# Tying ScalarE's order at the start and in the second output phase of a two-layer decoder step

## The chip, the core and the metric

The kernel runs on one core of one Trainium2 chip. The metric is the device time of one execution in microseconds (us), the median of several runs. Besides it there is one profiled execution, from which every duration and wait below is read; it has a time of its own.

The core has five engines with instruction queues of their own: TensorE (PE in the profile; its weight loads are PEld) multiplies matrices, VectorE (DVE), ScalarE (ACT) and GpSimd (POOL) work on elements, and SyncE (SP) issues transfers. ACT issues transfers too. Each engine works through its queue in order and waits on semaphores for the others.

## The reference

Two layers act on 1024 prompt tokens and 8 sample tokens, 1032 columns in all, with a model width of 1024. Cut to what matters here:

```
for i in range(2):                       # layer 0: HGRN2 recurrence, layer 1: gMLP
    hn = rmsnorm(h, norm_mix[i])
    y  = mixer_i(hn)                     # in-projection, mixer, gate, out-projection
    h  = h + y
    gate = sigmoid(rmsnorm(h, norm_ple[i]) @ w_ple_gate[i])
    h  = h + gate * (p[i] @ w_ple_proj[i])
out = rmsnorm(h, norm_final)
rmsnorm(x, g) = x * rsqrt(mean(x * x) + EPS) * g
```

The first rmsnorm squares x itself. The product p[i] @ w_ple_proj[i] needs only inputs, so it can run at any time.

## The kernel before, in words

**Numbers.** All is float32, and every product is made of three matmuls (`mm3`, L201 to L203): each operand is split into a high part (a cast on ACT, L196 for activations and L142 for weights) and a low part (a subtraction on DVE or POOL, L197 and L143).

**Tiling.** The columns are three chunks c = 0, 1, 2 of 384, 384 and 264. A projection of one output block for one chunk (`proj`) is 24 matmuls into one PSUM bank; a group of the p-projection (`pple`) is 6. `proj`, `pple` and the output phase share three banks with the tag "mm". A group of `pple` is copied out by ACT (L301) to a buffer `pple_t`, and a transfer that ACT itself issues (L302) stores it in DRAM (`ppd`). So the fourth group after a copy that is late waits for it.

**What sets the order.** PE's order is the program's order: the scheduler is told to leave PE alone. Small side jobs (the sum matmul `pss` of a norm, its broadcast `pbc`, the transposes `pt_g`) are generators in a clock called `Ticks`: a yield of n means that the next step stands n ticks later, and a tick falls at half of a projection, at its end, or behind `pple` groups. SQD, SDEL and NDEL are such delays. On ACT, DVE, POOL and SP a scheduler chooses the order from its estimates of time, and the order is then fixed.

**Start (0 to 50 us).** p and x are loaded; 12 `pple` groups run; meanwhile `first_norm` (L382 on) squares each chunk of x in four pieces on ACT (L386, POOL adds them for chunks 1 and 2, L387 and L389), `pss` adds over partitions, `pbc` spreads the scale, and DVE writes x times scale (`tmp`, L270), ACT casts it (`bh<-tmp`) and DVE or POOL subtract (`bl`). Then come the projections f (`fk`) and q (`qq`) of the first head, chunk by chunk.

**Layer 0 (to 880), p-projection and gate (to 1058), then the middle (1058 to 1121).** In the middle 12 `pple` groups of layer 1 run under the last gate work, `norm_rows` (NDEL[1]) makes the chunks' norms, `vgroup` applies gelu (L945) to six value projections and puts their transposes (`vstore`, L954) two ticks later, and `mix` combines rows of h on DVE and POOL (L905 to L908) whose casts are `xmh<-h`.

**Units (1121 to 1643), then the second output phase, "ob" (1643 to 1780).** Gated products are stored in `ozd` (L1155), loaded back and split for the output projection `ps_o`. `out_phase` runs the last 12 `pple` groups as filling while its operands come: `load_zt` loads two blocks at a time into three buffers `zstg` and splits each at once (`load_split`, L306). Before that, the last unit loads blocks singly into the tiles `u` (`fetch`) and casts them to `xmh` and `bh`; the fetches (1,4) and (1,8) stand there last, eight single blocks.

The prediction's steps are in `first_norm`, `pple`, `load_zt`, `out_phase` and `vgroup`.

Of the kernel before, what the change touches and what calls it, by code (L numbers as in the profile page):

```python
# [7 lines left out]
F32 = mybir.dt.float32  # L8
# [8 lines left out]
P = 128  # L17
# [12 lines left out]
PRI = 400  # L30
NWARM = 12
FDEL = ((2, 2), (2, 4), (1, 3))
SQD = (0, 5, 9)
OD = (4, 4)
SDEL = ((6, 3), (6, 2), (6, 2))
NDEL = (((1, 3), (1, 4), (2, 3)), ((2, 4), (2, 6), (2, 6)))
OFF = (0, 384, 768)
W = (384, 384, 264)
NT = (3, 3, 2)
# [37 lines left out]
def trunk_kernel(ctx, tc, xT, st, pT, nrm, wina, lbl, gna, wouta, winb, lng, lnb, lngr, lnbr,  # L77
# [7 lines left out]
    def pool(stack, name, bufs=1, **kw):  # L85
        return stack.enter_context(tc.tile_pool(name=name, bufs=bufs, reuse_waits="tile", **kw))
# [105 lines left out]
        return loaded[n]  # L192


    def split(hi, lo, src, eng=V):
        A.copy(hi, src)  # L196
        eng.tensor_tensor(lo, src, hi.bitcast(F32), ALU.subtract)  # L197

    def mm3(ps, wh, wl, xh, xl, first, last, more=False):
# [81 lines left out]
        return ps  # L281


    def load_p(ap, l, c, ph, pl):
        stg = ap.tile([P, 2, 384], F32, name="pstg", bufs=2)
        nc.sync.dma_start(stg[:, :, :W[c]], pT[l][:, :, OFF[c]:OFF[c] + W[c]])
        ph[c] = ap.tile([P, 2, W[c]], F32R, name=f"ph{c}")
        pl[c] = ap.tile([P, 2, W[c]], F32R, name=f"pl{c}")
        split(ph[c], pl[c], stg[:, :, :W[c]], V)

    def pple(l, tp, ph, pl, half, stg):

        wh, wl = take("p", l, half)
        for c in CH:
            for mm in range(4):
                ps = pp.tile([P, 512], F32, name="ps_pple", tag="mm", bufs=3)
                for k in range(2):
# [3 lines left out]
                A.copy(t[:, :W[c]], ps[:, :W[c]])  # L301
# [18 lines left out]
    def run(gen):  # L320
        for _ in gen:
            pass
# [43 lines left out]

    load(0)
    ph, pl = [None] * 3, [None] * 3
    load_p(sp, 0, 0, ph, pl)
    load_p(sp, 0, 1, ph, pl)  # L370
    load_x(0)
    nc.sync.dma_start(ones, cst[1])
    nc.sync.dma_start(ident, cst[0])
    nc.sync.dma_start(g32, nrm)
    load_p(sp, 0, 2, ph, pl)
    load_x(1)
    load(1)
    load_x(2)
# [1 line left out]
    fill = pple(0, sp, ph, pl, 0, ("pple_t", 4))  # L380

    def first_norm(c):  # L382
        yield SQD[c]
        sq = sp.tile([P, KT, 384], F32, name="sq0", bufs=2)[:, :, :W[c]]
        for j in range(0, KT, 2):
            A.activation(sq[:, j:j + 2, :], xs[c][:, j:j + 2, :], AF.Square)  # L386
            (V if c == 0 else G).tensor_tensor(sq[:, j, :], sq[:, j, :], sq[:, j + 1, :], ALU.add)  # L387
            if j:
                (V if c == 0 else G).tensor_tensor(sq[:, 0, :], sq[:, 0, :], sq[:, j, :], ALU.add)  # L389
        yield from norm_proc(sp, sq[:, 0, :], lambda j: xs[c][:, j, :], 0, hh[c], hl[c], c, SDEL[c])  # L390

# [382 lines left out]
    def out_phase(key, zt, ssq, first, done, pre, parts, late, fill=None):  # L774

        with ExitStack() as s:
            zp = pool(s, "oz")

            def load_h(m):
                if m < KT:  # L780
                    src = xT[:, m] if first else hd[m]
                    for c in CH:
                        nc.sync.dma_start(hr[c][m], src[:, OFF[c]:OFF[c] + W[c]])

            st = stage2(pool(s, "zstg"), 3)
            for c, k0, nk in parts:
                zt[c, k0] = (zp.tile([P, nk, W[c]], F32R, name=f"zh{c}_{k0}"),
                             zp.tile([P, nk, W[c]], F32R, name=f"zl{c}_{k0}"), nk)
            todo = load_zt(zt, late, st)
            if fill is not None:  # L790
                for i, _ in enumerate(fill):
                    if i % 2:
                        tk.tick()
                        next(todo, None)
                run(load_zt(zt, [(2, 0)], st))
            run(todo)
            for m in range(4):
                load_h(m)

            def bank():  # L800
                return pp.tile([P, 512], F32, name="ps_o", tag="mm", bufs=3)

            def half(ps, wt, c, hf):
                for _ in out_half(ps, wt, zt, c, hf):
                    tk.tick()

            def add(m, c, ps):
                V.tensor_tensor(hr[c][m], hr[c][m], ps[:, :W[c]], ALU.add)  # L808
                accum_sq(sp, ssq[c], hr[c][m], m == 0, m == KT - 1, W[c])
                if m == KT - 1:  # L810
                    done(c)


            wt = pre["w"] if pre else take(key, 0, 0)
            for c in CH:
                if c not in pre:
                    pre[c] = bank()
                    half(pre[c], wt, c, 0)
            wt = take(key, 1, 0)
            pre1 = [pp.tile([P, 384], F32, name="ps_o1", tag=t, bufs=1) for t in ("pA", "po", "pt")]  # L820
            for c in CH:
                half(pre1[c], wt, c, 0)
            for m, pm in ((0, pre), (1, pre1)):
                wt = take(key, m, 1)
                for c in CH:
                    half(pm[c], wt, c, 1)
                    add(m, c, pm[c])
            for m in range(2, KT):
                wts = [take(key, m, hf) for hf in range(2)]
                load_h(m + 2)  # L830
                for c in CH:
                    ps = bank()
                    for hf in range(2):
                        half(ps, wts[hf], c, hf)
                    add(m, c, ps)
# [103 lines left out]
    def wide():  # L939
        return wb.tile([P, 384], F32, name="u", bufs=6)  # L940

    def vgroup(m, c, src):
        w = W[c]
        gv = wide()
        A.activation(gv[:, :w], src, AF.Gelu_apprx_tanh)  # L945
# [219 lines left out]
    for g in range(8):  # L1165
        us = {}
        unit(take("B", 2 * g), gated(us))
        vn = wb2.tile([P, 8, DV], F32, name="vn", bufs=1)
        nc.sync.dma_start(vn, vraw[g])
        for n in range(8):  # L1170
            V.tensor_scalar(vn[:, n, :], vn[:, n, :], mv[:, n, 0:1], ln["rstd"][:, n:n + 1], ALU.subtract, ALU.mult)
        gb = wb2.tile([P, 2, DV], F32, name="gb", bufs=1)
        nc.sync.dma_start(gb[:, 0, :], lngr[g].partition_broadcast(P))
        nc.sync.dma_start(gb[:, 1, :], lnbr[g].partition_broadcast(P))
        cv = wb2.tile([P, DV], F32, name="cv", bufs=1)
        G.tensor_tensor(cv, vn[:, 7, :], gb[:, 0, :], ALU.mult)
        G.tensor_tensor(cv, cv, gb[:, 1, :], ALU.add)
        nc.sync.dma_start(cv_p[:, g * DV:(g + 1) * DV], cv)
        if g < 7:
            spatial(g, vn, us, take("B", 2 * MI + 2 * g))  # L1180
        else:

            zt = {(0, 0): (hh[0], hl[0], 8), (1, 0): (*xm[1], 4), (1, 4): (*xm[0], 4), (1, 8): (*xm[2], 4),
                  (0, 8): (hh[1], hl[1], 8), (2, 0): (hh[2], hl[2], 8)}
            ph, pl = p_in_act(1, None, False)

            def fetch(c, k0):
                return lambda: run(load_zt(zt, [(c, k0)], lambda w: wide()[:, :w].rearrange("p (k t) -> p k t", k=1), 1))

            spatial(g, vn, us, take("B", 2 * MI + 2 * g),  # L1190
                    (lambda: p_in_act(1, lambda w: ws[0].tile([P, 512], F32, name="ssum", bufs=2)[:, :w]), None, fetch(1, 0), fetch(0, 0), fetch(1, 4),
                     fetch(1, 8)))
# [111 lines left out]
```

## Time and profile before

| | us |
|---|---|
| median of three runs | 1976.65 |
| runs | 1976.61, 1976.65, 1980.89 |
| the profiled execution, its own time | 1973.68 |
| its span (first to last instruction) | 1971.9 |
| TensorE busy | 1893.8 (96%) |
| VectorE, ScalarE, GpSimd busy | 1182.6, 782.9, 456.8 |

The span leaves out 1.78 us of the profiled execution's time (1973.68 - 1971.9). In the profile's rows `L301` is line 301 of the kernel before; "A <- B" means that A's engine sat idle until B released it; a shape as 128x384 is partitions by elements. PEclk is the clock that was granted to TensorE, 1.00 being full speed.

### The profile page before, as it was taken

The page shows a single profiled execution, that of the slowest core. Times are in us where ns is not written, and L with a number is a line of the kernel's source. Part 1 is how long each engine was busy: PE and PEld are TensorE (multiplying, and loading weights), DVE is VectorE, ACT ScalarE, POOL GpSimd, SP SyncE. Part 2 cuts the span into 40 slices and gives each one's busy share as a digit, 9 for nine tenths or more (in the row PEclk, how much of TensorE's full clock was granted, in tenths as well). Part 3 has the DMA queues.
Part 4 walks back from the last instruction along what each step waited for, and adds up shares of the span by engine and source line. Part 5 has one row for each costly group of instructions (what it writes and reads, how often), then busy time and mean ns, then how long its engine had stood idle before and what let it go on. Part 6 is the DMA issues. An engine that isn't in the chain of part 4 may idle for free.

```text
span 1971.9 us, 33475 instructions
## 1 busy us (share of the span) xinstructions
PE 1893.8 (96%) x13160; PEld 1852.3 (94%) x13160; DVE 1182.6 (60%) x2610; ACT 782.9 (40%) x1610; POOL 456.8 (23%) x467
## 2 busy tenths in 40 slices
PE   7999999999999998999998899999999996999997
PEld 6999999999999998999998899999999996999997
DVE  5967676776767676311645755587777675311554
ACT  6452535444453536311434544433443344211341
POOL 5110000001000100011323622354444440011221
PEclk8999999999999999999999899999999998999998
DMA  6232322222131326511243333332233238411123
GB/s 207 84 105 71 101 91 79 76 89 97 57 108 59 106 93 217 185 44 44 98 157 111 108 98 92 102 98 95 97 99 105 95 113 262 138 49 44 65 87 107
DMA packets 124076, 203.73 MB, mean 103 GB/s; under 512 B 11600, under 2 KB 96784, under 8 KB 122896
## 3 DMA queue, kind: packets, MB, share of 16 engines
q1 hardware_dynamic: 115280, 191.04, 29.9%
q10 hardware_dynamic: 8640, 10.57, 1.5%
q8 instruction: 103, 1.69, 0.4%
q14 instruction: 53, 0.43, 0.1%
HBM read 148.75 MB, written 52.82 MB: 102 GB/s over the span
## 4 chain that ended last, share of the span: by engine, by line
PE 45%; DVE 7%; DMA 4%; issue 2%; POOL 2%; ACT 2%; SPq 0%; DVEq 0%; POOLq 0%; ACTq 0%
PE ps_proj L202 7%; PE ps_proj L201 7%; PE ps_proj L203 7%; PE ps_o L201 6%; PE ps_o L202 6%; PE ps_o L203 6%; PE ps_d L201 1%; PE ps_d L203 1%; PE ps_d L202 1%; DMA zstg<-ozd 1%; DVE wlo L143 1%; DMA vn<-vraw 1%; DVE bl L197 1%; PE psp L1139 1%; DMA ppd<-pple_t 1%
## 5 line engine op out<-in xcount | busy, mean ns | idle before, releaser
L201 PE MATMUL ps_proj<-bh,whi 128*128 128x384 f32 (+1 forms) x2136 | 689.2, 323 | 8.1 <-ACT pple_t L301 6.7
L202 PE MATMUL ps_proj<-bl,whi 128*128 128x384 f32 (+1 forms) x2136 | 673.3, 315 | 3.8 <-DVE bl L197 2.5
L203 PE MATMUL ps_proj<-bh,wlo 128*128 128x384 f32 (+1 forms) x2136 | 672.9, 315 | 3.1 <-DVE wlo L143 3.1
L201 PEld LDWEIGHTS ps_proj<-bh,whi 128*128 128x128 f32 x2136 | 404.3, 189 | 12.2 <-ACT pple_t L301 6.9
L202 PEld LDWEIGHTS ps_proj<-bl,whi 128*128 128x128 f32 x2136 | 404.8, 190 | 6.6 <-DVE bl L197 3.4
L203 PEld LDWEIGHTS ps_proj<-bh,wlo 128*128 128x128 f32 x2136 | 403.6, 189 | 3.7 <-DVE wlo L143 3.7
L143 DVE TENSOR_TENSOR wlo<-wstg,whi 128x1024 fp32r<-128x1024 f32 x148 | 190.7, 1289 | 152.1 <-ACT whi L142 148.8
L142 ACT CAST whi<-wstg 128x1024 fp32r<-128x1024 f32 x148 | 155.3, 1050 | 130.0 <-PE ps_proj L202 72.3
L234 POOL TENSOR_TENSOR ssq<-ssq,tmp 128x384 f32<-128x384 f32 (+1 forms) x72 | 76.3, 1059 | 419.9 <-ACT tmp L233 372.2
L808 DVE TENSOR_TENSOR h<-h,ps_o 128x384 f32<-128x384 f32 (+1 forms) x48 | 24.5, 511 | 192.9 <-PE ps_o L203 192.9
L142 ACT CAST shi<-ssum 128x512 fp32r<-128x512 f32 x92 | 56.5, 621 | 176.9 <-POOL ssum L172 102.7
L201 PE MATMUL ps_o<-bh,whi 128*128 128x384 f32 (+1 forms) x384 | 123.2, 321 | 2.1 <-ACT pple_t L301 1.6
L202 PE MATMUL ps_o<-bl,whi 128*128 128x384 f32 (+1 forms) x384 | 122.6, 319 | 0.6 <-DVE bl L197 0.6
L233 ACT ACTIVATE tmp<-h 128x384 f32<-128x384 f32 (+1 forms) x72 | 35.3, 490 | 219.5 <-DVE h L808 168.9
L203 PE MATMUL ps_o<-bh,wlo 128*128 128x384 f32 (+1 forms) x384 | 122.4, 319 | 0.0
L143 DVE TENSOR_TENSOR slo<-ssum,shi 128x512 fp32r<-128x512 f32 x92 | 76.7, 833 | 42.9 <-ACT shi L142 42.9
L201 PE MATMUL ps_o<-zh,whi 128*128 128x384 f32 (+1 forms) x288 | 90.0, 313 | 0.0
L202 PE MATMUL ps_o<-zl,whi 128*128 128x384 f32 (+1 forms) x288 | 89.7, 312 | 0.0
L203 PE MATMUL ps_o<-zh,wlo 128*128 128x384 f32 (+1 forms) x288 | 89.7, 311 | 0.0
L589 DVE TENSOR_TENSOR q<-q,t 128x192 f32<-128x192 f32 (+1 forms) x144 | 49.9, 347 | 45.2 <-PE pC L583 43.5
L201 PEld LDWEIGHTS ps_o<-bh,whi 128*128 128x128 f32 x384 | 72.7, 189 | 2.8 <-ACT pple_t L301 2.1
L202 PEld LDWEIGHTS ps_o<-bl,whi 128*128 128x128 f32 x384 | 72.6, 189 | 1.0 <-DVE bl L197 1.0
(278 smaller groups left out, 3904.1 us busy)
## 6 DMA issues: line engine op xcount, KB each, us to landing
wstg<-in_wina SPq DMA_DIRECT2D x48, 512.0 KB, 3.6
wstg<-in_winb SPq DMA_DIRECT2D x48, 512.0 KB, 4.0
zstg<-ozd SPq DMA_DIRECT2D x22, 384.0 KB, 5.7
pj<-ppd SPq DMA_DIRECT2D x16, 516.0 KB, 3.8
S<-in_st SPq DMA_DIRECT2D x16, 512.0 KB, 5.1
vb<-vd SPq DMA_DIRECT2D x16, 512.0 KB, 4.6
out_so_s<-S SPq DMA_DIRECT2D x16, 512.0 KB, 3.4
wstg<-in_wouta SPq DMA_DIRECT2D x16, 512.0 KB, 4.2
```

Of the source, the lines that this page charges most:

```text
L142: A.copy(hi, src)
L143: V.tensor_tensor(lo, src, hi.bitcast(F32), ALU.subtract)
L197: eng.tensor_tensor(lo, src, hi.bitcast(F32), ALU.subtract)
L201: PE.matmul(ps, wh, xh, start=first, stop=False, skip_group_check=more)
L202: PE.matmul(ps, wh, xl, start=False, stop=False, skip_group_check=more)
L203: PE.matmul(ps, wl, xh, start=False, stop=last, skip_group_check=more)
L233: A.activation(sq[:, :w], src, AF.Square)
L234: eng.tensor_tensor(ssq, ssq, sq[:, :w], ALU.add)
L589: V.tensor_tensor(ql[:, :, 1, :], ql[:, :, 1, :], t2[:, :, 0:1].broadcast_to([P, n, lv]), ALU.mult)
L808: V.tensor_tensor(hr[c][m], hr[c][m], ps[:, :W[c]], ALU.add)
L1139: PE.matmul(pss[:, i, :], vn[:, n0 + i, mm * P:(mm + 1) * P], wst[:, g, :], start=True, stop=True)
```

## The change

Three places. At the start, the squares of chunks 1 and 2 are one per tick, and each is tied on ACT behind the copy of `pple` (chunk 1) or the cast of a split (chunk 2) that the program wrote last; the delays SQD and SDEL are others, and p has three staging buffers instead of two. In the output phases, `load_zt` separates loads from casts (in "ob" by two steps), its casts keep the program's order on ACT, each `pple` group takes a step of it and ticks, and the blocks (1,4) and (1,8) move from the last unit into "ob" as two-block loads. In the middle, the transposes stand four ticks behind their gelu instead of two, and the norm of chunk 2 starts a tick later.

```diff
-SQD = (0, 5, 9)
+SQD = (0, 7, 12)
-SDEL = ((6, 3), (6, 2), (6, 2))
-NDEL = (((1, 3), (1, 4), (2, 3)), ((2, 4), (2, 6), (2, 6)))
+SDEL = ((6, 4), (1, 2), (0, 2))
+NDEL = (((1, 3), (1, 4), (2, 3)), ((2, 4), (2, 6), (3, 6)))
 def split(hi, lo, src, eng=V):
-        A.copy(hi, src)
+        last["split"] = A.copy(hi, src)
 def pple(l, tp, ph, pl, half, stg):
-                A.copy(t[:, :W[c]], ps[:, :W[c]])
+                last["pple"] = A.copy(t[:, :W[c]], ps[:, :W[c]])
-    def load_zt(zt, parts, stage, n=2):
-        for c, k0 in parts:
-            zh, zl, nk = zt[c, k0]
-            for k in range(0, nk, n):
-                load_split(zh[:, k:k + n, :], zl[:, k:k + n, :], ozd[c][:, k0 + k:k0 + k + n, :], stage(W[c]))
-                yield
+    def load_zt(zt, parts, stage, n=2, lag=0):
+        todo = [(c, k0, k) for c, k0 in parts for k in range(0, zt[c, k0][2], n)]
+        stg = []
+        for i in range(len(todo) + lag):
+            if i < len(todo):
+                c, k0, k = todo[i]
+                stg.append(stage(W[c]))
+                nc.sync.dma_start(stg[i], ozd[c][:, k0 + k:k0 + k + n, :])
+            if i >= lag:
+                c, k0, k = todo[i - lag]
+                zh, zl, _ = zt[c, k0]
+                tc.keep_in_program_order(A.copy(zh[:, k:k + n, :], stg[i - lag]))
+                V.tensor_tensor(zl[:, k:k + n, :], stg[i - lag], zh[:, k:k + n, :].bitcast(F32), ALU.subtract)
+            yield
 def first_norm(c):
-        yield SQD[c]
+        if c:
+            yield SQD[c]
         for j in range(0, KT, 2):
-            A.activation(sq[:, j:j + 2, :], xs[c][:, j:j + 2, :], AF.Square)
+            with tc.issue_after(last["pple" if c == 1 else "split"].ins) if c else ExitStack():
+                A.activation(sq[:, j:j + 2, :], xs[c][:, j:j + 2, :], AF.Square)
+            if c:
+                yield 1
 def out_phase(key, zt, ssq, first, done, pre, parts, late, fill=None):
+            st = stage2(pool(s, "zstg"), 3)
             zp = pool(s, "oz")
-            st = stage2(pool(s, "zstg"), 3)
-            todo = load_zt(zt, late, st)
-            if fill is not None:
-                for i, _ in enumerate(fill):
-                    if i % 2:
-                        tk.tick()
-                        next(todo, None)
-                run(load_zt(zt, [(2, 0)], st))
+            todo = load_zt(zt, late, st, 2, 2 if fill else 0)
+            for _ in fill or ():
+                next(todo, None)
+                tk.tick()
             run(todo)
-    def vgroup(m, c, src):
+    def vgroup(m, c, src, d=2):
-        tk.spawn(vstore(m, c, gv), 2)
+        tk.spawn(vstore(m, c, gv), d)
-            vgroup(m, c, ps[:, :W[c]])
+            vgroup(m, c, ps[:, :W[c]], 4)
-                    (lambda: p_in_act(...), None, fetch(1, 0), fetch(0, 0), fetch(1, 4),
-                     fetch(1, 8)))
+                    (lambda: p_in_act(...), None,
+                     fetch(1, 0), fetch(0, 0)))
-              [(1, 12, 4), (2, 8, 8)], [(0, 8), (1, 12), (2, 8)], pple(1, sp, ph, pl, 1, ("tmp", 4)))
+              [(1, 12, 4), (2, 8, 8)], [(1, 4), (1, 8), (0, 8), (2, 0), (1, 12), (2, 8)], pple(1, sp, ph, pl, 1, ("tmp", 4)))
```

ScalarE while the norms of chunks 1 and 2 are made, before (`bh0` and `bh2` are the high parts of chunks 0 and 2, `sq0<-xs2` a square of chunk 2):

```order
L196 CAST bh0_120<-tmp_330 128x384
L386 ACTIVATE sq0_350<-xs2_137 128x2x264
L196 CAST bh0_120<-tmp_334 128x384
L386 ACTIVATE sq0_350<-xs2_137 128x2x264 x2
L196 CAST bh0_120<-tmp_338 128x384
L196 CAST bh0_120<-tmp_342 128x384
L386 ACTIVATE sq0_350<-xs2_137 128x2x264
L196 CAST bh0_120<-tmp_346 128x384
```

All four squares of chunk 2 stood among the casts of chunk 0. Now the last square of chunk 1 (`sq0<-xs1`) stands behind the fifth cast of chunk 0:

```order
L198 CAST bh0_120<-tmp_339 128x384
L400 ACTIVATE sq0_282<-xs1_136 128x768
L198 CAST bh0_120<-tmp_343 128x384
L303 COPY pple_t_365<-ps_pple_358 128x264
L198 CAST bh0_120<-tmp_347 128x384
L198 CAST bh0_120<-tmp_351 128x384
```

And the last two squares of chunk 2 stand behind the eighth cast of chunk 1 (`bh1`), which itself is behind the gate `sg` of the first q projection:

```order
L198 CAST bh1_121<-tmp_451 128x384
L436 ACTIVATE sg_502<-ps_proj_474 128x384
L198 CAST bh1_121<-tmp_455 128x384
L198 CAST bh1_121<-tmp_459 128x384
L198 CAST bh1_121<-tmp_463 128x384
L198 CAST bh1_121<-tmp_467 128x384
L400 ACTIVATE sq0_388<-xs2_137 128x2x264 x2
L423 ACTIVATE f_543<-ps_proj_518 128x384
```

On PE six matmuls of `pple` stood between the `pss` of chunk 1 and the first projection, and now none do; the `pss` of chunk 2 stood behind 36 matmuls of projections and now stands behind 48.

ScalarE where the second output phase begins, before:

```order
L196 CAST xmh2_11490<-u_18627 128x384
L1152 ACTIVATE sg_18689<-u2_18481 128x384
L196 CAST xmh2_11490<-u_18631 128x384
L196 CAST xmh2_11490<-u_18635 128x384
L196 CAST xmh2_11490<-u_18639 128x384
L196 CAST bh1_11499<-zstg_18772 128x768
L301 COPY pple_t_18759<-ps_pple_18752 128x384
L301 COPY pple_t_18769<-ps_pple_18762 128x384
L302 DMA ppd1_4_88<-pple_t_18759 128x384
```

and now:

```order
L142 CAST whi_18716<-wstg_18714 128x1024
L1165 ACTIVATE sg_18657<-u2_18481 128x384
L303 COPY pple_t_18727<-ps_pple_18720 128x384
L303 COPY pple_t_18739<-ps_pple_18732 128x384
L304 DMA ppd1_4_88<-pple_t_18727 128x384
L304 DMA ppd1_5_89<-pple_t_18739 128x384
L303 COPY pple_t_18751<-ps_pple_18744 128x384
L304 DMA ppd1_6_90<-pple_t_18751 128x384
L324 CAST xmh0_11486<-zstg_18730 128x768
L303 COPY pple_t_18765<-ps_pple_18758 128x384
```

The eight casts `xmh<-u` and the first cast `bh<-zstg` no longer stand ahead of the first copies out of PSUM; four two-block casts `xmh<-zstg` stand between later copies.

More of the change, by code (lines that the diff above doesn't have):

```diff
@@ L192, in take @@
         return loaded[n]
+    last = {}
     def split(hi, lo, src, eng=V):
-        A.copy(hi, src)
+        last["split"] = A.copy(hi, src)
         eng.tensor_tensor(lo, src, hi.bitcast(F32), ALU.subtract)
@@ L281, in proj, with load_p @@
         return ps
-    def load_p(ap, l, c, ph, pl):
-        stg = ap.tile([P, 2, 384], F32, name="pstg", bufs=2)
+    def load_p(ap, l, c, ph, pl, bufs=2):
+        stg = ap.tile([P, 2, 384], F32, name="pstg", bufs=bufs)
         nc.sync.dma_start(stg[:, :, :W[c]], pT[l][:, :, OFF[c]:OFF[c] + W[c]])
@@ L368, in trunk_kernel @@
     ph, pl = [None] * 3, [None] * 3
-    load_p(sp, 0, 0, ph, pl)
-    load_p(sp, 0, 1, ph, pl)
+    load_p(sp, 0, 0, ph, pl, 3)
+    load_p(sp, 0, 1, ph, pl, 3)
     load_x(0)
@@ L374, in trunk_kernel @@
     nc.sync.dma_start(g32, nrm)
-    load_p(sp, 0, 2, ph, pl)
+    load_p(sp, 0, 2, ph, pl, 3)
     load_x(1)
@@ L1190, in trunk_kernel @@
             spatial(g, vn, us, take("B", 2 * MI + 2 * g),
-                    (lambda: p_in_act(1, lambda w: ws[0].tile([P, 512], F32, name="ssum", bufs=2)[:, :w]), None, fetch(1, 0), fetch(0, 0), fetch(1, 4),
-                     fetch(1, 8)))
+                    (lambda: p_in_act(1, lambda w: ws[0].tile([P, 512], F32, name="ssum", bufs=2)[:, :w]), None,
+                     fetch(1, 0), fetch(0, 0)))
     sB.close()
```

## The prediction

> **What bounds the kernel now.** I read the engines' shares first, then the waits of TensorE over the whole span, then the windows in which these waits lie.
>
> ```profile
> PE 1893.8 (96%) x13160; PEld 1852.3 (94%) x13160; DVE 1182.6 (60%) x2610; ACT 782.9 (40%) x1610; POOL 456.8 (23%) x467
> ```
>
> TensorE is the bound, at 96%. The change adds and removes no matmul, so it can only move TensorE's idle time, or the time at a lower clock. The waits say who ends that idle time (us in total, times, longest):
>
> ```profile
> PE ps_pple L201 <- ACT pple_t L301: 21.4, 8, 12.8
> PE pss L246 <- DVE ssq L231: 7.7, 2, 4.3
> PE ps_proj L201 <- ACT pple_t L301: 6.7, 1, 6.7
> PE pt_g L954 <- ACT u L945: 6.6, 2, 4.0
> PE ps_proj L203 <- DVE wlo L143: 3.1, 2, 2.8
> ```
>
> These are 45.5 us, 2.3% of the span, and the first, third and fourth rows end at ScalarE. The windows put a clock beside them (us; then busy time and count of PE, PEld, DVE, ACT, POOL; granted clock, DMA share, GB/s):
>
> ```profile
> 27.07:37.31 10.24, 3.71 (x12) 3.71 (x13) 7.36 (x13) 6.38 (x13) 10.01 (x12) 0.50 0.25 91
> 1092.03:1098.86 6.83, 5.12 (x17) 5.13 (x18) 6.83 (x12) 5.33 (x12) 6.83 (x7) 0.50 0.10 29
> 1648.40:1662.06 13.66, 2.90 (x9) 2.90 (x10) 7.36 (x13) 6.92 (x14) 0.99 (x1) 0.50 0.79 260
> ```
>
> After a long wait TensorE has half its clock for a while. Busy time in such a window is worth half, so the second window costs 2.6 us beyond the wait and the third 1.45.
>
> **The second output phase ("ob"): the largest wait.** TensorE stands 12.82 us here, and ScalarE shows why:
>
> ```profile
> 1649.07 1.56 ACT L196 CAST xmh<-u 128x384 fp32r<-128x384 f32 x3 [1.29 <-DMA u<-ozd]
> 1650.67 0.52 ACT L1152 ACTIVATE sg<-u 128x384 f32<-128x384 f32 x1
> 1651.75 1.10 ACT L196 CAST xmh<-u 128x384 fp32r<-128x384 f32 x2 [0.55 <-DMA u<-ozd]
> 1653.20 0.51 ACT L196 CAST xmh<-u 128x384 fp32r<-128x384 f32 x1 [0.36 <-DMA u<-ozd]
> 1657.90 0.83 ACT L196 CAST bh<-zstg 128x768 fp32r<-128x768 f32 x1 [4.19 <-DMA zstg<-ozd]
> 1658.64 0.85 ACT L301 COPY pple_t<-ps_pple 128x384 f32<-128x384 f32 x2
> 1659.16 0.69 PE L201 MATMUL ps_pple<-bh,whi 128*128 128x384 f32 x1 [12.82 <-ACT pple_t L301]
> ```
>
> The first three groups filled three banks by 1646.35 (1659.16 - 12.82). Their copies stood behind casts of loaded tiles, the last of which waited 4.19 us for its transfer. In the new order nothing but `sg` is ahead of them. `sg` needs its multiplication (L1066), which comes right behind the s of L1141:
>
> ```profile
> 1647.00 0.61 DVE L1141 SCALAR_TENSOR_TENSOR s<-psp,lg,bt 128x384 f32<-128x384 f32 x1
> 1650.09 0.55 DVE L1066 TENSOR_TENSOR u<-ps_d,u 128x384 f32<-128x384 f32 x1
> ```
>
> So L1066 ends at about 1648.2, `sg` (0.52) at 1648.7, the first copy (0.48) at 1649.2: the wait becomes about 2.8 and 10.0 us are gained. They don't all stay. What is late next are transfers: the same eight blocks now come later, through three staging buffers on SP, and the casts tied between the copies wait for them; the copies reuse four buffers that the `ppd` transfers must have left.
>
> ```profile
> zstg<-ozd SPq DMA_DIRECT2D x5, 384.0 KB
> u<-ozd SPq DMA_DIRECT2D x8, 192.0 KB
> ppd<-pple_t ACTq DMA_DIRECT2D x3, 192.0 KB, 5.2
> 1662.06:1672.30 10.24, 7.39 (x47) 6.65 (x45) 2.05 (x3) 3.82 (x8) 0.00 (x0) 1.00 1.00 346
> ```
>
> A `ppd` took 5.2 us to land. Issued at 1649.2, the first frees its buffer at 1654.4, where the fifth copy would be ready at about 1652.5 (three more groups at 1.05 us each): some 2 us back. The fourth two-block cast needs its transfer: eight 192 KB blocks at 346 GB/s are 4.5 us of all transfers, behind what is under way, and I put it at 1661, 1 to 4 us after ScalarE could take it. I take 3.5 us back in all, of bounds 0 (all hidden behind groups) and 9 (every later load waits as the 4.19 and the first `ppd` did). Gain here 6.5, bounds 1 and 10.
>
> **The middle.** Here the waits are spread over three engines:
>
> ```profile
> 1070.17 0.70 PE L246 MATMUL pss<-ones,ssq 128*128 128x1 f32 x6 [3.36 <-DVE ssq L231]
> 1085.59 0.69 PE L203 MATMUL ps_proj<-bh,wlo 128*128 128x384 f32 x1 [2.75 <-DVE wlo L143]
> 1093.74 0.90 PE L954 MATMUL pt_g<-ident,u 128*128 128x128 f32 x3 [4.01 <-ACT u L945]
> ```
>
> The `pss` of chunk 2 now stands behind 12 more matmuls of 384 columns. Two neighbours in a free run start 0.17 us apart:
>
> ```profile
> 39.72 0.33 PE L201 MATMUL ps_proj<-bh,whi 128*128 128x384 f32 x1
> 39.89 0.33 PE L202 MATMUL ps_proj<-bl,whi 128*128 128x384 f32 x1
> ```
>
> So 12 are 2.1 us, and 3.36 becomes about 1.25. The transposes stand one projection (24 matmuls, 4.1 us) later, which covers the 4.01; but the same gelu also has to free a bank for the projection after, and it is itself behind mixing:
>
> ```profile
> 1086.42 0.51 ACT L196 CAST xmh<-h 128x384 fp32r<-128x384 f32 x1 [3.04 <-POOL h L907]
> 1091.37 0.51 ACT L196 CAST xmh<-h 128x384 fp32r<-128x384 f32 x1 [3.19 <-POOL h L907]
> 1091.90 1.28 ACT L945 ACT_TABLE_LOAD   x1
> 1093.19 0.49 ACT L945 ACTIVATE u<-ps_proj 128x384 f32<-128x384 f32 x1
> ```
>
> That order on ScalarE stays. I take 3 of the 4.01, nothing of the second wait of the same row (6.6 - 4.0 = 2.6) and of the `wlo` wait, and 1 of the 2.6 at half clock: 2.1 + 3 + 1 is a gain of about 6, bounds 2 (the `pss` alone) and 11 (all of 3.36 + 4.01 + 2.6, and 1 of the rest).
>
> **The start: a wait that goes and one that comes.**
>
> ```profile
> 21.14 0.39 PE L201 MATMUL ps_pple<-ph,whi 128*128 128x264 f32 x1 [2.77 <-ACT pple_t L301]
> 33.60 0.69 PE L201 MATMUL ps_proj<-bh,whi 128*128 128x384 f32 x1 [6.66 <-ACT pple_t L301]
> 42.31 0.63 PE L246 MATMUL pss<-ones,sq 128*128 128x1 f32 x6
> 47.14 0.92 PE L257 MATMUL pbc<-ident,rsq 128*128 128x128 f32 x6
> ```
>
> The 2.77 go, since the copies are now ahead of chunk 1's squares; but what sets the first projection is later. It stands directly behind the `pss` of chunk 1 now, and the last square of chunk 1 behind the fifth cast of chunk 0, at 28 to 29 instead of 19.88:
>
> ```profile
> 19.88 0.84 ACT L386 ACTIVATE sq<-xs 128x768 f32<-128x768 f32 x1 [1.58 <-DMA xs<-in_xT]
> 28.92 0.51 ACT L196 CAST bh<-tmp 128x384 fp32r<-128x384 f32 x1 [0.91 <-DVE tmp L270]
> ```
>
> Square (0.84) and two additions of 1 us on POOL put that `pss` at about 31.1 and the projection at 31.7, against 33.60: 1.9 us gained. Then the new wait. Before, the `pss` of chunk 2 stood at 42.31 without idle time, its squares made under the casts of chunk 0. Now its last two squares stand behind the eighth cast of chunk 1. This cast needs the `pbc` of chunk 1, which stands behind 24 matmuls of f instead of 12, at about 38 (31.7, at half clock to about 37.3, then full). Before, from that `pbc` (about 37.5) to the last cast it took until 44.9:
>
> ```profile
> 44.41 0.52 ACT L196 CAST bh<-tmp 128x384 fp32r<-128x384 f32 x1
> L386 ACT ACTIVATE sq<-xs 128x528 f32<-128x528 f32 x4 | 2.4, 636 | 0.0
> L387 POOL TENSOR_TENSOR sq<-sq 128x264 f32<-128x264 f32 x4 | 3.7, 919 | 0.0
> L389 POOL TENSOR_TENSOR sq<-sq 128x264 f32<-128x264 f32 x3 | 3.3, 1095 | 0.2
> ```
>
> So squares at about 45 to 46.3, then four additions in a row on POOL, 2 x 0.92 + 2 x 1.1 = 4.0: the `pss` can start at about 49. TensorE has done its 48 projection matmuls by about 43: it waits 6 us where it waited none. Everything behind is queued: the f of chunk 1, then the `pbc` of chunk 2. Matmul 60 of the projections was done at 47.14; now it is 49 + 0.6 + 12 x 0.17 = 51.7, and 1.7 more if the wait brings another 3.41 us at half clock, which is likely: the row of 27.07 followed a wait of 6.66. I take +6, bounds +1 (additions at their fastest and squares slipped forward) and +11.5 (additions at their slowest, two half-clock windows, and the casts of chunk 2, covered by 24 matmuls instead of 36, late too). The third staging buffer saves nothing: the same transfers fill the start (323 GB/s below).
>
> ```profile
> 0.00:27.07 27.07, 19.86 (x102) 17.14 (x102) 12.92 (x25) 17.06 (x28) 9.45 (x13) 1.00 0.96 323
> ```
>
> The Trainium skill ("TensorE: Matmul & The Clock Gate", section "HAM oscillation") speaks against this edit: an idle window of about 3.4 us takes TensorE to half clock, and it must be busy as long to get the full one back. The trace agrees: its half-clock rows are 10.24, 6.83 and 13.66 us long, multiples of 3.41, and the 2.77 us wait at 21.14 brought none. By this rule the new 6 us wait costs 1.7 more; without it the start would be +4.6 instead of about +6.
>
> **The first output phase (742 to 880).** Casts and copies change places on ScalarE, matmuls don't. Its waits for copies are one of 1.7 and one of 1.6:
>
> ```profile
> PE ps_pple L201 <- ACT pple_t L301: 1.7, 1, 1.7
> PE ps_o L201 <- ACT pple_t L301: 1.6, 1, 1.6
> ```
>
> I take 0, bounds -2 and +3; the casts moved behind the last copies have the output matmuls of two chunks as cover.
>
> **The sum.** +6 - 6 - 6.5 + 0 = -6.5: 1967.2 against the profiled execution's 1973.68. The median of the runs shown is 1976.65, 3.0 above it, so I predict 1970.
>
> **The rivals.**
>
> *The start is cheap.* If squares and additions of chunk 2 slip ahead, or POOL takes its fastest additions, the start ends at about 0 and the time is 1976.65 - 12.5 = 1964. For it: POOL's durations scatter with what runs beside it. Against: the tie fixes the order on ScalarE.
>
> *The transfers take the gain of "ob" back.* Then it is worth 1 instead of 6.5: 1975.5. For it: the DMA share of 1.00 from 1662 to 1672 and the 4.19. Against: as many bytes were moved before.
>
> *The sum of chunk 2 decides (slower).* One mechanism: the tied squares make TensorE wait at the `pss` of chunk 2 by the upper bound, +11.5. It decides where the two other places give less than 5.6 us together; with their lower bounds, 3, it is +8.5: 1985. For it: nothing else is left for TensorE to do there. Against: both others must be near their lower ends.
>
> *The change does less than it says.* In the middle the gelu behind the mixing decides, not the place of the transposes: gain 2, time 1974. I count it in the forecast's range.
>
> **How the numbers follow.** The forecast has 0.48, a cheap start 0.22, transfers 0.12, slower 0.18. A measurement tells about 0.3% (5.9 us) from no change. The forecast's own range is 1964 to 1976, of which 0.26 is faster and 0.22 the same; a cheap start is faster, the transfers case the same, of the last 0.15 slower and 0.03 the same. Together faster 0.48, same 0.37, slower 0.15. The range goes from 1959 (a cheap start and good gains) to 1982.
>
> **What would show it.** In the changed profile: the 12.8 row of `ps_pple` falls to about 3, with new rows of 1 to 4 us behind it; the `pss` of chunk 2 at the start has a wait of about 6 for a square on POOL, and half clock after it; the wait of 3.36 falls near 1.3 and the 4.01 vanishes or becomes a wait of `ps_proj` for `u`. It is wrong if the new `pss` wait is under 3, or if "ob" still waits over 6 for its first copy.

## The result

The changed kernel is slower: 1987.56 us against 1977.1 us, medians of 8 runs each (the 1976.65 above is the median of the first three); the ratio is 1.0051, with a 95% interval of 1.0035 to 1.0067. The profiled execution took 1982.79 us (span 1981.1), against 1973.68 before. In the changed kernel's rows the helpers' line numbers are higher by two or more: L203 to L205 are the three matmuls of a product, L303 the copy of a `pple` group, L304 its store, L248 the sum `pss`, L324 the casts of `load_zt`, L400 the squares of x, L403 and L405 their additions.

TensorE's busy time, and its waits over the whole span, of the changed kernel (us in total, times, longest):

```profile
PE 1903.0 (96%) x13160; PEld 1858.9 (94%) x13160; DVE 1188.4 (60%) x2606; ACT 782.0 (39%) x1606; POOL 457.0 (23%) x467
```

```profile
PE pss L248 <- POOL sq L405: 15.1, 2, 8.5
PE ps_pple L203 <- ACT pple_t L303: 13.1, 10, 3.3
PE pt_g L967 <- ACT u L969: 7.2, 4, 4.5
PE pss L248 <- DVE ssq L233: 4.9, 2, 4.3
PE ps_proj L205 <- DVE wlo L143: 4.0, 2, 3.7
PE ps_o L203 <- ACT bh L324: 3.6, 1, 3.6
```

The 12.8 us wait of `ps_pple` and the 6.7 us wait of `ps_proj` for `pple_t` are gone. The wait for GpSimd's additions of squares, 1.0 us in all before, is 15.1 us now, in two places. The same matmuls have 9.2 us more busy time (1903.0 - 1893.8): more of them ran at half clock (the windows follow below).

**Where the time went, by stage.** I cut each profiled execution at six places that all kernels have: the first wait of `pt_o` (about 149 us), the first `ps_o` of the first output phase (779), the wait of `ps_pple` at the start of the middle (1062), the wait of `ps_proj` for `u` in the units (1287), TensorE's stop at the start of "ob" (1646), and the first `ps_proj` that waits for GpSimd's `bl` (1861); the last column goes to the end of TensorE's last matmul, 9.3 to 10.1 us ahead of the span's end. The output matmuls `ps_o` of the kernel before stand from 778.5 to 961 and from 1672.6 to 1857.5, so the ends 880 and 1780 given above for the two output phases are too early, and the column "ob" ends three us behind the last of them. The column "middle" goes on into the units. Stage lengths in us:

| kernel | start | layer 0 | to middle | middle | units | ob | rest |
|---|---|---|---|---|---|---|---|
| before | 148.7 | 629.8 | 283.8 | 225.1 | 358.9 | 214.3 | 101.8 |
| changed | 158.9 | 631.2 | 283.8 | 222.7 | 357.7 | 214.8 | 102.5 |
| k1 start as before | 152.0 | 634.3 | 283.8 | 222.6 | 357.1 | 214.6 | 101.8 |
| k2 chunk 2 untied | 151.2 | 634.2 | 285.6 | 222.6 | 357.3 | 215.1 | 102.4 |
| k3 output phases alone | 150.0 | 632.7 | 284.2 | 225.1 | 357.1 | 212.9 | 102.1 |
| k4 middle alone | 150.9 | 628.6 | 284.2 | 224.2 | 358.6 | 216.9 | 102.2 |
| k5 k1, first output phase untied | 152.3 | 632.9 | 285.4 | 222.6 | 357.4 | 211.7 | 102.5 |
| k6 k5, late h in ob | 150.2 | 631.7 | 285.4 | 222.6 | 357.5 | 200.5 | 101.7 |
| k7 k5, stores by GpSimd | 150.2 | 632.0 | 285.5 | 222.7 | 358.0 | 210.9 | 102.1 |
| k8 k5, stores by SyncE | 149.6 | 632.6 | 283.8 | 222.6 | 358.5 | 207.3 | 102.1 |
| k9 before, late h in ob | 151.3 | 628.5 | 284.2 | 226.1 | 357.4 | 208.7 | 101.8 |
| k10 k6, pool order as before | 149.5 | 629.8 | 283.8 | 222.6 | 357.4 | 202.4 | 102.2 |
| k11 k10, stores by SyncE | 149.9 | 629.3 | 285.3 | 222.7 | 359.6 | 204.0 | 102.1 |
| k12 k10, sums' casts late | 150.6 | 629.0 | 284.6 | 222.0 | 357.9 | 203.0 | 102.2 |

Each row is one execution; that of the changed kernel is the fastest of its eight, 4.8 us under their median, and that of k3 the fastest of its ten, 5.5 under theirs. The column "start" says how far one can trust a row: the twelve kernels with the old start lie from 148.7 to 152.3. The changed one's 158.9 is outside of that.

**The start.** TensorE's two waits, ScalarE's casts and squares, and GpSimd's additions ahead of the second wait, from the timelines of the changed kernel:

```profile
32.34 1.44 PE L248 MATMUL pss<-ones,sq 128*128 128x1 f32 x6 [8.45 <-POOL sq L405]
51.96 1.14 PE L248 MATMUL pss<-ones,sq 128*128 128x1 f32 x6 [6.68 <-POOL sq L405]
```

```profile
45.32 0.49 ACT L436 ACTIVATE sg<-ps_proj 128x384 f32<-128x384 f32 x1 [1.25 <-PE ps_proj L205]
45.71 2.04 ACT L198 CAST bh<-tmp 128x384 fp32r<-128x384 f32 x4
47.66 1.17 ACT L400 ACTIVATE sq<-xs 128x528 f32<-128x528 f32 x2
```

```profile
48.52 1.05 POOL L403 TENSOR_TENSOR sq<-sq 128x264 f32<-128x264 f32 x1
49.65 0.74 POOL L405 TENSOR_TENSOR sq<-sq 128x264 f32<-128x264 f32 x1
50.35 0.74 POOL L403 TENSOR_TENSOR sq<-sq 128x264 f32<-128x264 f32 x1
51.17 0.74 POOL L405 TENSOR_TENSOR sq<-sq 128x264 f32<-128x264 f32 x1
```

The chain reads downward: `sg` waits for the q projection, the last four casts of chunk 1 wait behind `sg`, the tied squares behind the casts, four additions behind the squares, the sum behind the additions. TensorE had stopped at 45.28.

**ob.** ScalarE at its start in the changed kernel:

```profile
1656.59 0.84 ACT L303 COPY pple_t<-ps_pple 128x384 f32<-128x384 f32 x2
1657.08 1.23 ACTq L304 DMA_DIRECT2D ppd<-pple_t  x2
1658.35 0.48 ACT L303 COPY pple_t<-ps_pple 128x384 f32<-128x384 f32 x1 [0.92 <-DMA zstg<-ozd]
1663.52 0.33 ACTq L304 DMA_DIRECT2D ppd<-pple_t  x1
1663.89 0.83 ACT L324 CAST xmh<-zstg 128x768 fp32r<-128x768 f32 x1 [5.06 <-DMA h<-hd]
1664.62 0.47 ACT L303 COPY pple_t<-ps_pple 128x384 f32<-128x384 f32 x1
```

The first copies come 2.8 us after TensorE's stop. Then ScalarE does nothing from 1658.83 to 1663.52: the third store of `ppd` is next in its queue and is issued only at 1663.52; behind it stand the cast and the fourth copy. In these microseconds SyncE issues nine loads of h, whose first row is not used before 1711.27, and the next load of `zstg` comes behind them:

```profile
1659.34 6.51 SPq L800 DMA_DIRECT2D h<-hd  x9
1665.97 0.41 SPq L320 DMA_DIRECT2D zstg<-ozd  x1
```

The windows of the changed kernel at half clock (us; busy time and count of PE, PEld, DVE, ACT, POOL; granted clock, DMA share, GB/s):

```profile
25.14:38.79 13.65, 6.45 (x22) 6.45 (x23) 7.82 (x16) 8.28 (x16) 12.02 (x12) 0.50 0.41 149
49.03:55.86 6.83, 3.90 (x15) 3.87 (x16) 0.21 (x2) 0.00 (x0) 3.57 (x5) 0.50 0.00 0
...
1656.71:1660.12 3.41, 3.02 (x9) 3.02 (x10) 2.13 (x3) 1.20 (x3) 0.02 (x1) 0.50 0.68 155
1666.95:1670.37 3.42, 3.27 (x12) 2.96 (x11) 1.33 (x2) 0.97 (x2) 0.00 (x0) 0.50 0.97 352
1673.78:1680.61 6.83, 6.13 (x22) 5.82 (x22) 2.88 (x3) 3.59 (x7) 0.00 (x0) 0.50 1.00 326
1694.26:1697.67 3.41, 3.41 (x13) 3.41 (x12) 2.89 (x4) 2.35 (x3) 0.00 (x0) 0.50 0.85 237
```

Before, TensorE idled through most of its long half-clock window in ob (2.90 us busy in 13.66), and one short window was full; now all of them are nearly full. The short one before:

```profile
1672.30:1675.71 3.41, 3.41 (x12) 3.14 (x12) 0.96 (x1) 1.62 (x4) 0.00 (x0) 0.50 1.00 308
```

### The profile page after: what moved, and what is told of

It is laid out like the page before. It is cut to its first block, busy times and chain, and to the rows that moved or that the text cites. A ratio compares the mean times of both kernels' runs of the same rounds, so it can differ in the third digit from the quotient of the medians.

```text
span 1981.1 us, 33462 instructions
## 1 busy us (share of the span) xinstructions
PE 1903.0 (96%) x13160; PEld 1858.9 (94%) x13160; DVE 1188.4 (60%) x2606; ACT 782.0 (39%) x1606; POOL 457.0 (23%) x467
## 4 chain that ended last, share of the span: by engine, by line
PE 41%; DVE 8%; DMA 4%; issue 3%; ACT 2%; POOL 2%; SPq 0%; DVEq 0%; ACTq 0%; POOLq 0%
PE ps_proj L204 6%; PE ps_proj L203 6%; PE ps_proj L205 6%; PE ps_o L203 6%; PE ps_o L204 6%; PE ps_o L205 6%; DMA wstg<-in_winb 2%; DVE wlo L143 1%; PE ps_d L203 1%; PE ps_d L205 1%; PE ps_d L204 1%; DMA zstg<-ozd 1%; DVE bl L199 1%; DVE tmp L272 1%; PE pt_g L967 1%
## 5 line engine op out<-in xcount | busy, mean ns | idle before, releaser
L203 PE MATMUL ps_proj<-bh,whi 128*128 128x384 f32 (+1 forms) x2136 | 689.8, 323 | 0.0
L205 PE MATMUL ps_proj<-bh,wlo 128*128 128x384 f32 (+1 forms) x2136 | 673.6, 315 | 4.0 <-DVE wlo L143 4.0
L203 PEld LDWEIGHTS ps_proj<-bh,whi 128*128 128x128 f32 x2136 | 404.8, 190 | 4.1 <-issue 2.5
L205 PEld LDWEIGHTS ps_proj<-bh,wlo 128*128 128x128 f32 x2136 | 403.8, 189 | 4.9 <-DVE wlo L143 4.9
L203 PE MATMUL ps_o<-bh,whi 128*128 128x384 f32 (+1 forms) x384 | 124.0, 323 | 4.7 <-ACT bh L324 3.6
L205 PE MATMUL ps_o<-bh,wlo 128*128 128x384 f32 (+1 forms) x384 | 123.2, 321 | 0.0
L203 PE MATMUL ps_o<-zh,whi 128*128 128x384 f32 (+1 forms) x288 | 90.0, 313 | 0.0
L205 PE MATMUL ps_o<-zh,wlo 128*128 128x384 f32 (+1 forms) x288 | 89.7, 311 | 0.0
L203 PEld LDWEIGHTS ps_o<-bh,whi 128*128 128x128 f32 x384 | 73.4, 191 | 5.1 <-ACT bh L324 3.8
```

Source lines behind the costliest of these rows:

```text
L203: PE.matmul(ps, wh, xh, start=first, stop=False, skip_group_check=more)
L205: PE.matmul(ps, wl, xh, start=False, stop=last, skip_group_check=more)
```

## The experiments

Ratios are to the kernel before, with the 95% interval. In the expectations, "first mark to ps_o" counts from TensorE's stop ahead of the first mark, which is 1.0 to 1.6 us more than the table's column.

**Which place makes the loss?** k1 puts SQD, SDEL and `first_norm` back (the third staging buffer of p stays, in k3 too). k3 has the output phases alone, k4 the middle alone.

```diff
 # k1: the changed kernel with
-SQD = (0, 7, 12)
+SQD = (0, 5, 9)
-SDEL = ((6, 4), (1, 2), (0, 2))
+SDEL = ((6, 3), (6, 2), (6, 2))
 # and first_norm as before; k3: also d=4 and NDEL as before; k4: d=4 and NDEL alone
```

> The changed kernel with the start (SQD, SDEL, first_norm) as before; the middle and the output phases stay changed. Theory A (the start alone makes the loss; from the two traces' offsets it is +9.6 us at 157): the time comes back to the kernel before within about 1 us, since the other places give -2.4 in the middle, about +2.5 at the first output phase and +0.5 in ob. Rival B (the loss is spread, the later stages carry it too): it stays over 4 us above the kernel before. By the prediction's other terms (-6 and -6.5) it would be 12 us faster than before.

1.0000 (0.9991 to 1.0010), 1976.44 us. The start makes the whole loss; the other two places together neither gain nor lose.

> Only load_zt and the output phases changed; start and middle as before. Theory A (the 12.8 us wait is cut into several short ones, and half clock falls on busy time): first wait of ob about 3 us, 3 to 5 us faster in waits there but no faster at the end of ob (-1 to +1), and +1 to +3 at the first output phase; 0 to +4 over the kernel before. Rival B (as predicted, ob gains 6.5): 4 to 7 us faster than before.

1.0019 (1.0010 to 1.0029), 1980.86 us. In the table, from its fastest execution: ob 1.4 us shorter, the units 1.8, layer 0 2.9 longer. Theory A's size holds, with ob a little outside its -1 to +1; the predicted gain isn't there.

> Only the middle changed (transposes four ticks late, norm of chunk 2 a tick later). Theory A (the gelu behind the mixing decides, only the pss wait goes): -2 to -3 us. Rival B (as predicted): -6 us, the 4.01 us wait gone.

0.9996 (0.9981 to 1.0010), the stage 0.9 us shorter. That is under both numbers; in all kernels that have the output phases' change too, the middle is 2.4 to 3.1 us shorter. So the change is worth 1 to 3 us, and by the interval, which ends at a gain of 3.8 us, the predicted 6 is excluded.

**What in the start?** k2 leaves the changed start in place, except that the squares of chunk 2 are no longer tied.

```diff
-            with tc.issue_after(last["pple" if c == 1 else "split"].ins) if c else ExitStack():
+            with tc.issue_after(last["pple"].ins) if c == 1 else ExitStack():
                 A.activation(sq[:, j:j + 2, :], xs[c][:, j:j + 2, :], AF.Square)
```

> The changed kernel with one tie left out: the squares of chunk 2 are not tied behind the last cast of a split, and on ScalarE they move, the last two of them, from behind the eighth cast of chunk 1 to ahead of the first sigmoid; TensorE's order is the changed one. Theory A (the tie makes the second wait at the start): the 6.68 us wait of the third pss falls under 0.5, the half clock after it (49.03 to 55.86) goes, and the time is 7 to 10 us under the changed kernel, +1 to +3 over the one before. Rival B (the place of that pss in TensorE's order, or the additions on GpSimd, make it): the wait stays over 3 us and less than 4 us are gained.

1.0015 (1.0005 to 1.0025), 1979.13 us: 8.4 us below the changed kernel's median, 7.1 by the ratios. Its ScalarE row and its waits of the first 60 us:

```profile
35.92 1.71 ACT L400 ACTIVATE sq<-xs 128x528 f32<-128x528 f32 x3
37.65 1.28 ACT L423 ACT_TABLE_LOAD   x1
```

```profile
PE pss L248 <- POOL sq L405: 9.0, 1, 9.0
```

Three squares run at 35.92, ahead of the first sigmoid, and the wait of the third `pss` is gone; that of the second, 9.0, stays. TensorE's order is the changed one, so it was the tie, not the place of `pss`. Of what k1 wins back, 11 us by the medians and 10 by the ratios, the tie has 7 to 8. What remains (some 3 us between k1 and k2) belongs to the rest of the changed start; no run divides it.

**Why does ob give nothing?** k5 is k1 with the casts of the first output phase untied. It is the base of k6 to k8. k6 issues the 24 loads of h in ob behind the last load of `zstg`; k7 and k8 let GpSimd or SyncE issue the stores of `ppd`. k9 is the kernel before with late h.

```diff
 # k5
-                tc.keep_in_program_order(A.copy(zh[:, k:k + n, :], stg[i - lag]))
+                cp = A.copy(zh[:, k:k + n, :], stg[i - lag])
+                if lag:
+                    tc.keep_in_program_order(cp)
 # k6 and, in load_split, k9
+                last["zt"] = nc.sync.dma_start(stg[i], ozd[c][...])
+                        with tc.issue_after(last["zt"].ins) if fill else ExitStack():
                             nc.sync.dma_start(hr[c][m], src[:, OFF[c]:OFF[c] + W[c]])
 # k7 (k8: nc.sync)
-                nc.scalar.dma_start(ppd[l][4 * half + mm]...
+                (nc.gpsimd if l and half else nc.scalar).dma_start(ppd[l][4 * half + mm]...
```

> The changed kernel with the start as before and, in the first output phase, the casts of load_zt no longer tied to the program's order (in ob they stay tied). Theory A (the tied casts at the end of layer 0 hold back the small ACT work that po waits for, and the wait of 2.2 us and its half clock follow): from the first mark (about 150) to the first ps_o matmul the profile is 630 to 632 us as in the kernel before instead of 635 to 636, and the time is 2 to 4 us under that of the kernel before. Rival B (separating loads from casts, not the tie, costs it): no change there, within 1 us of the kernel before.

1.0008 (0.9998 to 1.0018), and 634.4 us from the stop ahead of the first mark to `ps_o`. Theory A fell here: untying the casts makes the stage 1.4 us shorter than k1's, less than single executions differ, and the time no shorter. See k10.

> As k5, and in ob the 24 loads of h are issued only behind the last load of zstg. Theory A (ob is bound by its transfers: the DMA share is 0.97 to 1.00 and 4.2 MB of h, some 12 us at 350 GB/s, stand between the loads that ps_o waits for): the waits of ps_o and ps_pple after the first one fall from about 9 us to under 4, ob gains 4 to 7 us against k5. Rival B (ScalarE's own issues of ppd, which wait for older transfers, hold the copies back): under 2 us are gained.

0.9931 (0.9916 to 0.9946), 1961.91 us, and ob takes 200.5 us instead of 211.7. Its waits and a window in ob:

```profile
PE ps_pple L203 <- ACT pple_t L303: 5.3, 3, 2.5
PE ps_o L204 <- DVE bl L327: 0.2, 1, 0.2
```

```profile
1660.00:1672.00 12.00, 10.76 (x68) 10.54 (x67) 6.46 (x7) 6.37 (x12) 0.00 (x0) 1.00 0.89 260
```

The waits fell to 5.5 us in all and full clock returns at 1653. The gain, 11.2 us in the stage, is above the 4 to 7 expected; by the ratios the whole kernel gains 15, and the rest of that lies in stages that the edit doesn't touch. The h rows were loaded long before their use, between loads that TensorE waited for. ScalarE's standing at its third store goes too; here the copy and the store follow each other:

```profile
1650.84 0.48 ACT L303 COPY pple_t<-ps_pple 128x384 f32<-128x384 f32 x1 [0.51 <-ACT pple_t L303]
1651.35 0.33 ACTq L304 DMA_DIRECT2D ppd<-pple_t  x1
```

> As k5, and the 12 stores of ppd in ob are issued by GpSimd instead of ScalarE. Theory B (ScalarE stands in a ppd issue, from 1658.4 to 1663.5 in the changed kernel, and copies and casts behind it wait): the 3 us wait of ps_pple after the first goes, ob gains 2 to 4 us. Theory A (transfers bind): it gains under 1.5 us, since the waits move to the copies that reuse a buffer, or to the casts.

0.9984 (0.9974 to 0.9994): about 4.7 us against k5 by the ratios, while ob is only 0.8 us shorter in the one execution that was profiled. I take no size from it. The wait of `ps_pple` after the first, which theory B said would go, is 6.05 us there, behind a cast that waits 6.35 us for `zstg`: the wait moved, as theory A said.

> As k5, and the 12 stores of ppd in ob are issued by SyncE. Theory B: as with GpSimd if SyncE is free, 2 to 4 us; but SyncE's queue also holds the loads of zstg and h, each of which may wait, so 0 to 2 us. Theory A: under 1.5 us.

0.9966 (0.9956 to 0.9976), ob 4.4 us shorter than in k5. More than either theory gave, but it doesn't separate them: with the stores in SyncE's queue the loads of h come later too, three of them before 1670 where k5 has thirteen. So theory A can make this gain as well, and theory B is not shown; k11 tests it with h late.

> The kernel before with one edit: in ob the 24 loads of h are issued only behind the last load of zstg. Theory A (the loads of h stand between the loads that ob waits for, in both kernels): the 12.8 us first wait stays within 2 us (its casts wait for u and the first zstg, ahead of h), the later ones go, 2 to 5 us faster than before; then k6 minus this one, some 7 to 11 us, is what the change of ob is worth once its transfers are free. Rival C (late h alone is the gain, the change of ob adds nothing): 12 us or more faster than before.

0.9971 (0.9962 to 0.9981), 1970.79 us. Its waits from 1640 to 1700:

```profile
PE ps_pple L201 <- ACT pple_t L301: 13.4, 2, 12.8
```

The 12.8 us wait stays, and late h alone gains 5.0 us by the medians, the upper end of the expectation. In ob k6 is 8.2 us shorter than k9, k10 6.3 and k12 5.7: the change of ob is worth 6 to 8 us once the loads that nobody waits for yet are out of the way.

**The first output phase, and a best version.** k10 is k6 with the old order of the two pools where there is no filling; k11 adds SyncE's stores.

```diff
-            st = stage2(pool(s, "zstg"), 3)
+            if fill:
+                st = stage2(pool(s, "zstg"), 3)
             zp = pool(s, "oz")
+            if not fill:
+                st = stage2(pool(s, "zstg"), 3)
```

> As k6 (h late), and in the first output phase the pool zstg is opened behind oz as in the kernel before, which gives the order of loads there back. Theory D (the pool's place lets three loads of the first output phase start among the last loads of layer 0, and ppd and casts wait for them): from the first mark (about 150) to ps_o 630 to 631 us instead of 633 to 636, 2 to 4 us faster than k6. Rival (run-to-run place of the half-clock windows): within 1 us of k6.

0.9923 (0.9906 to 0.9941), 1961.27 us, not distinguishable from k6 by its time, so the 2 to 4 us are not shown there. By the profiles the theory holds (631.3 us from the stop ahead of the first mark): with the pool opened first (eight kernels), layer 0 takes 631.2 to 634.3 us; with the old order (six kernels), 628.5 to 629.8. The two sets don't meet. The waits from 740 to 790, of k5 and then of k10:

```profile
PE po L203 <- ACT junk L631: 2.3, 1, 2.3
PE ps_o L203 <- ACT pple_t L303: 2.1, 1, 2.1
```

```profile
PE ps_o L203 <- ACT pple_t L303: 1.5, 1, 1.5
PE pos L730 <- ACT junk L631: 1.0, 1, 1.0
PE po L203 <- ACT junk L631: 0.4, 1, 0.4
```

With the pool opened first, three loads of the first output phase stand earlier in SyncE's order, ahead of a load of weights (`wstg`, issued at 765.36 in k6 and 760.70 in k10) and of layer 0's last stores. What ScalarE then waits for was not taken apart.

> As k10, and the stores of ppd in ob issued by SyncE. Theory B beside A (ScalarE's own issues hold copies back also with free transfers): 1 to 3 us faster than k10. Otherwise, or if SyncE's queue holds the stores back: within 1 us of k10 or slower.

0.9932 (0.9910 to 0.9954): no gain over k10. With h late, ScalarE's issues cost nothing that shows, so theory B has no run for it beyond k7's time.

**The middle.** TensorE's longest wait there in the changed kernel, and ScalarE ahead of it:

```profile
1123.13 0.90 PE L967 MATMUL pt_g<-ident,u 128*128 128x128 f32 x3 [4.47 <-ACT u L969]
```

```profile
1118.32 0.49 ACT L958 ACTIVATE u<-ps_proj 128x384 f32<-128x384 f32 x1
1122.08 0.62 ACT L142 CAST shi<-ssum 128x512 fp32r<-128x512 f32 x1 [3.28 <-POOL ssum L174]
1122.61 0.47 ACT L969 COPY u<-pt_g 128x384 f32<-128x384 f32 x1
```

The gelu (L958) is in time now. The transposes wait for the copy of the transposes before them, as there is one bank for them, and this copy is queued behind a cast that waits for GpSimd. k12 ties those casts behind.

```diff
-        A.copy(gt[:, :NT[c], :], pt[:, :NT[c], :])
+        last["vst"] = A.copy(gt[:, :NT[c], :], pt[:, :NT[c], :])
...
-    load(taken[0])
+    with tc.issue_after(last["vst"].ins):
+        load(taken[0])
```

> As k10 (start as before, middle and ob changed, h late, pool order of the first output phase as before), and in the middle ScalarE's casts for the first unit's weights (shi<-ssum, whi) are tied behind the third last copy of transposed values. Theory E (in the changed middle the wait of 4.47 us is for a copy L969 that stands behind a cast waiting 3.28 us for ssum from GpSimd): this wait falls under 1.5 us, the middle takes 219 to 221 us instead of 222.6, 1 to 4 us faster than k10. Rival (the casts are then late for the first unit, or DVE's mixing ends the wait as well): a wait of ps_proj for slo or wlo takes its place, within 1 us of k10.

0.9929 (0.9907 to 0.9952), the middle 222.0 us against 222.6 in k10. The waits in the middle:

```profile
PE pt_g L968 <- ACT u L970: 6.1, 3, 2.4
PE ps_proj L205 <- DVE wlo L143: 4.5, 2, 3.7
```

The longest wait, 4.5 in k10 too, went down to 2.4, and the row from 8.4 us in k10 to 6.1; theory E said under 1.5. The rival has the time right, within 1 us of k10, and not the cause: the row for `wlo` was 4.3 in k10 and is 4.5, so it took nearly nothing. Half clock took more: its windows in the middle hold 8.8 us of work, against 6.7 in k10, which costs 1.1 more. What would free the middle stays open.

## Why the prediction was wrong

Forecast 1970 in 1959 to 1982; measured 1987.56. Term by term, from the table: start +6, measured +8.5; middle -6, measured -2.4; ob -6.5, measured +0.5; first output phase 0, measured about +3.5. These are +10.1 in place of -6.5. The slower rival, with 0.18, is the nearest: its wait for the tied squares came, and the two other places gave less than its 5.6. Its own time, 1985, lay outside the range that I gave.

**The start, +6.** The tied squares made a wait of 6.68 where 6 was worked out, and k2 shows that the tie made it. Half clock followed it for 6.83 us with 3.90 busy, a loss of 1.95 where 1.7 stood. That the wait came out so near is in part luck, for both its ends came later: TensorE stopped at 45.28 instead of 43, and the sum started at 51.96 instead of 49. (The 49 was also added up short: squares to 46.3 and 4.0 of additions behind them are 50.3. The additions took 3.4, from 48.52 to 51.91, so the slowest additions of the upper bound did not happen.) The step that failed is "1.9 us gained". The projections were to start at 31.7 against 33.60. GpSimd was at a subtraction until 30.06 when the last square of chunk 1 was done (29.70), the second `pss` started at 32.34 instead of 31.1 and ran at half clock, and the first projection started at 33.64. Half clock reached from 25.14 to 38.79 with 6.45 us of work in it, where before it was 10.24 us with 3.71; that takes 1.4 us more. The stage's +8.5 is 158.9 against a mean near 150 in the twelve executions with the old start; the medians of the changed kernel and of k1 differ by 11.1. I had put +6 and left +11.5 to a rival.

**ob, -6.5.** The first wait became 2.81, as worked out (2.8). The failed step is "I take 3.5 us back": later waits grew from 4.0 to 10.3 us (the profile's gaps after the first, added up), and half clock fell on 15.8 us of work instead of 6.3, which costs 4.8 more. So -10.0 + 6.3 + 4.8 = +1.1; the stage grew by 0.5. The 3.5 reckoned with the blocks of `ozd` and the stores of `ppd`; the loads of h stood in no term, and half clock behind the shorter waits was put at nothing without a reason. The rival of the transfers had 0.12 and was right about this place. My argument against it was that as many bytes moved before; but before, they moved during the long wait, and now they move during work. k6 against k9 shows it from the other side: with the 24 loads of h behind, the same edit gains 6 to 8 us.

**The clock step.** The trace's rule was used for the new wait at the start only. It speaks of ob too: one 12.8 us wait had most of its half clock inside itself, and several waits of 2 to 4 us have it on work. I had named the long window as a cost of 1.45 us, and gave the shorter waits none.

The Trainium skill ("TensorE: Matmul & The Clock Gate", section "What's actually happening") says that the window is free-running. The traces agree: the half-clock windows start on one grid of 3.41 us (27.07 and 1071.55 are 306 windows apart).

**The middle, -6.** The `pss` step held: 3.36 became 0.58 in the changed kernel's profile. "I take 3 of the 4.01" failed: the wait for the gelu went, and one of 4.47 for the copy of the former transposes came, which I had not looked for. The stage gained 2.4, near the 2 of the rival "does less than it says", though not by its mechanism: the gelu behind the mixing did not decide.

**The first output phase, 0.** It cost about 3.5 us (632.7 against 629.2 on the mean of the two sets), above the bound of 3. I looked at the casts' order; k5 and k10 show that it was the place of a pool, which moved loads.

## What to carry to other kernels

Before tying work that feeds a sum on the bound engine's path behind a later stage, follow the whole chain behind the tied instruction: here two squares of 0.6 us held TensorE 6.7 us, as casts of the other chunk stood ahead of them and four additions behind. A long wait on TensorE can be a cover for transfers and for the half clock; whoever removes it should first look which transfers are not needed yet and put them behind those that are. A row of loads that is merely early can cost more than the wait that one sees: late h alone gave 0.29% (k9), and with the changes of ob and the middle, the old start and the old order of the pools 0.77% (k10).

## What was not expected of the hardware

Waits shorter than a 3.41 us window brought half clock, and others did not. In k6 TensorE stopped from 1647.53 to 1650.00, 2.47 us, and this window follows:

```profile
1649.60:1653.01 3.41, 3.01 (x9) 3.01 (x10) 2.57 (x4) 2.42 (x5) 0.04 (x1) 0.50 0.80 204
```

In the kernel before a 2.77 us wait at 18.37 brought none. In k1 one of 2.49 us at 20.09, in the same place of the program, was followed by half clock from 23.93 to 27.35. TensorE's busy time in the grid window that ends where half clock begins doesn't sort them either: 1.34 us of 3.41 in k6 (1646.19 to 1649.60) and 1.65 in k4 (974.74 to 978.16) were followed by half clock, 1.54 in the kernel before (16.83 to 20.24) was not. What decides stays open; the 3.4 us of idle time in the prediction's rule is too mild for these runs.

So the same start can cost different amounts from one execution to the next. Among the twelve executions with the old start, the four with 17.07 us of half clock in it (k1, k4, k5, k9) are the four longest, 150.9 to 152.3; the eight with 6.83 to 13.65 us lie from 148.7 to 150.6. That this makes all of the spread was not shown.

ScalarE's issue of a store can stand for 4.7 us (1658.83 to 1663.52) while the DMA share is 0.97 (the window 1660 to 1664 of the changed kernel), and everything behind it in ScalarE's queue stands as well. With the loads of h out of the way, in k6, the same store is issued right behind its copy (1651.35).
